# Hybrid attention and mLSTM encoder layer: ScalarE by hand in the attention stage, two normalizations shared by two engines, two mask additions moved

## The chip, the cores and the metric

The kernel runs on one core of one Trainium2 chip. The metric is the device time of one execution in microseconds (us), measured over several runs; lower is better.

## What is computed

One layer of an encoder on 2048 tokens of width 1024, in float32. The input is normalized, scaled and shifted by vectors made from a conditioning vector, and projected. The columns of the projection feed two groups of heads, whose outputs are normalized, concatenated, projected back, and followed by a SwiGLU feed-forward part. Cut to what matters here:

```python
hmix = rms_norm(x, g_norm1) * (1.0 + scale1) + shift1
q_a, k_a, v_a, q_m, k_m, v_m, o_m, gates = split(hmix @ w_in)
# 8 heads of 64 in two groups of 4; |t - s| <= 128, so a block of 128 queries sees up to 3 blocks of keys
logits = where(valid, scores - slopes * dist, -inf)
mx  = maximum(max(logits), sink)
p   = exp(logits - mx); den = sum(p) + exp(sink - mx)
att = rms_norm((p / den) @ v, g_attn_out)
# 4 heads of 128, chunks of 128, a forward and a backward scan, added
h_m = rms_norm(mlstm_forward + mlstm_backward, g_mlstm_out) * sigmoid(o_m)
x = x + gate1 * (concatenate([att, h_m]) @ w_out)
# then the feed-forward part and the last norm
```

## The kernel before

TensorE (PE) does all products; VectorE (DVE), ScalarE (ACT) and GpSimd (POOL) share the rest; loads and stores are issued by SyncE (SP). Products that need float32 accuracy are made of three: a factor is split into a half rounded to the format of the fast product (made by ACT) and the remainder (made by DVE or POOL). The stages follow one another: modulation and first norm with the natural projections, gates, mLSTM, attention, output projection, feed-forward part.

**What sets the order.** Each engine works through its own queue in order. The framework schedules: from the program it lets each engine take whatever its model of the time says is ready, the earlier emitted first, and so may move an instruction far ahead of where it was emitted. Inside `tc.manual_schedule(engines=...)` the engines named keep the order of emission. PE is under it everywhere; the gates and mLSTM stages, and the output projection, hold all engines under it; in the attention stage of the kernel before, ACT, DVE, POOL and SP are left to the scheduler.

**The filler.** Projection matmuls (`gps`, L498) are generators in a deque, `fill`; `pull(n)` emits `n` of them between the other matmuls. A tile of 128 columns by 512 tokens takes 24 matmuls, and when the generator is resumed after the 24th, it emits the eviction by ACT (`qhi` of `qk_att`, `oth` of `o_tiles`). `put_soon(k, ...)` emits an operation `k` pulls later. `cols_steps` makes the weights of such a tile: the load of `wraw` (L247; there is one such buffer), the rounded half `whi` by ACT (L251), and the remainder `wlo` in four parts by POOL (L254). `next_cols` spreads these steps over the pulls ahead of their use; `proj_cols` emits all of them at once. `o_tiles` calls `proj_cols` when its first tile begins:

```python
        if not ws_:
            ws_.extend(proj_cols(C_OM + h * P) for h in heads)
```

In the attention stage the filler is: the rest of the sigmoid gate's head 0 (`o_first`), one query tile column (`second`), head 1 (`o_tiles((1,), ...)`), and heads 2 and 3 together, in four blocks (`lasts`).

**Attention.** 32 units (one block of 128 queries, one group of four heads) pass through a loop over `s_` with three stages in flight: the newest unit's four scores with DVE's maximum (L786) and ACT's exponential (L788); the normalization (`normalize`: a small ACT exponential, L794, two small DVE operations, and four scalings by POOL, L798) and, for the unit before, PE transposes (L805) with their split into `apth` (ACT, L141) and `aptl` (DVE, L142); and for the unit before that the products with the values (L817, L818) and their eviction `at` (L821, L822). The loop also draws on `first_pair`, from `s_` = 21 on one step each time: it loads the first pair of row tiles for the output projection, squares them on ACT (L1139) with additions on POOL (L1141, L1143), starts the loads of the first two parts of the output weights `wo` as soon as the filler's first block of heads 2 and 3 is done, and gates. After the loop `finish_wo` emits the halves of these weights (ACT L1046, DVE L1047).

**mLSTM.** For each of four heads a backward pass over the chunks 15 to 1 builds the backward states (`k_chunk`, `kv_mm`), then a forward pass makes scores, states and products. `load_bc` loads the rows of a chunk (`bc`), `prep` adds the mask to them on POOL (L629), `decays` takes the exponential on ACT (L635), and `scores` uses that. `prep` of chunks 0 and 1 is emitted after the backward pass.

Of the kernel before, what the change touches and what calls it, by code (L numbers as in the profile page):

```python
# [11 lines left out]
F32 = mybir.dt.float32  # L12
# [3 lines left out]
AF = mybir.ActivationFunctionType  # L16
ALU = mybir.AluOpType
MUL, ADD, SUB, MAX, MIN = ALU.mult, ALU.add, ALU.subtract, ALU.max, ALU.min
# [18 lines left out]
def hybrid_layer_kernel(  # L37
# [5 lines left out]
    pe, dve, act, pool, sp = nc.tensor, nc.vector, nc.scalar, nc.gpsimd, nc.sync  # L43
# [72 lines left out]
    def beat(k=1):  # L116
        for e in soon:
            e[0] -= k
        due = [e for e in soon if e[0] <= 0]
        soon[:] = [e for e in soon if e[0] > 0]  # L120
        for _, f, args in sorted(due, key=lambda e: e[0]):
            f(*args)

    def pull(n=1):

        while n > 0:
            if not fill:
                n -= 1
                beat()
            elif next(fill[0], None) is None:  # L130
                fill.popleft()
            else:
                n -= 1
                beat()

    def finish_fill(g):
        while any(f is g for f in fill):
            pull()
# [436 lines left out]
    def tick():  # L575

        due = [f for k, f in later if k <= 0]
        later[:] = [[k - 1, f] for k, f in later if k > 0]
        for f in due:
            f()  # L580

    def load_v(h, n):
        va = s2.tile([P, 4, 129], F32, tag="mv", name="mv", bufs=2)
        sp.dma_start(va, vaug_d[n * 512:(n + 1) * 512, h, :].rearrange("(c p) d -> p c d", p=P))
        return va

    def load_qk(h, j, n):
        t = s2.tile([P, 512], F32, tag="mqk", name="mqk", bufs=4)
        sp.dma_start(t, qk_d[j, h, n])
        return t  # L590

    def load_last(h):
        return {NB - 1: (load_qk(h, 1, NB - 1), load_v(h, NB - 1))}

    def mlstm(h, nb, nf, last):
# [5 lines left out]
        def load_bc(cc):  # L601
            bc = s2.tile([P, 4, P], F32, tag="bc", name="bc", bufs=3)
            sp.dma_start(bc.rearrange("p j t -> p (j t)"), bc_d[h, cc].rearrange("j t -> (j t)").partition_broadcast(P))
            return bc
# [3 lines left out]
        def k_chunk(k_c, va_c, d, cc):  # L608
            kn = kns.get(cc)
            if kn is None:  # L610
                tp = bank("a", "ktp")
                pe.transpose(tp[:, :P], k_c, ident)
                kn = kns[cc] = s2.tile([P, P], F32, tag=f"kn{cc}", name="kn", bufs=1)
                act.activation(kn, tp[:, :P], AF.Copy)
            vw = s2.tile([P, 129], F32, tag="vw", name="vw", bufs=4)
            rr = row(d, cc)
            act.activation(vw, va_c, AF.Copy, scale=wT[:, rr:rr + 1])
            return kn, vw

        def kv_mm(kn, vw, tag="a"):  # L620
            kvp = bank(tag, "kvp")
            pe.matmul(kvp[:, :129], kn, vw, start=True, stop=True)  # L622
            return kvp
# [3 lines left out]
        def prep(cc):  # L627
            ng = ngs[cc] = s2.tile([P, 2, P], F32, tag="ng", name="ng", bufs=3)
            pool.tensor_tensor(ng, bcs[cc][:, 0:2, :], maskb, ADD)  # L629

        def decays(cc):

            for d in range(2):
                rr = row(d, cc)
                act.activation(ngs[cc][:, d, :], ngs[cc][:, d, :], AF.Exp, bias=rT[:, rr:rr + 1])  # L635
# [5 lines left out]
        for cc in list(range(NT - 1, 0, -1)) + [0, 0, 0]:  # L641
            tick()
            n, i = divmod(cc, 4)
            if i == 3 and n and n - 1 not in blk:
                blk[n - 1] = (load_qk(h, 1, n - 1), load_v(h, n - 1))
            if cc == 6:
                q_first = load_qk(h, 0, 0)
            if cc in (6, 4, 2):
                bcs[3 - cc // 2] = load_bc(3 - cc // 2)
            if cc:  # L650
                todo.append((cc, *k_chunk(blk[n][0][:, i * P:(i + 1) * P], blk[n][1][:, i, :], 1, cc)))
                pull(nb - nb // 2)
            if len(todo) > 2 or (todo and not cc):
                c_, kn, vw = todo.popleft()
                kvp = kv_mm(kn, vw, "bcdc"[c_ % len("bcdc")])
                if c_ == NT - 1:
                    dve.tensor_copy(cb[:, c_ - 1, :], kvp[:, :129])
                else:
                    rr = row(1, c_)
                    dve.scalar_tensor_tensor(cb[:, c_ - 1, :], cb[:, c_, :], dec[:, rr:rr + 1], kvp[:, :129], MUL, ADD)  # L660
                pull(nb // 2)
        prep(0)
        prep(1)
        decays(0)


# [74 lines left out]
        for cc in range(NT + 1):  # L741
            tick()
            if cc == NT - 3 and h + 1 < HM:
                last = load_last(h + 1)
# [24 lines left out]
    class Unit:  # L769
# [18 lines left out]
            act.activation(p[:, :NK], p[:, :NK], AF.Exp, bias=nm, scale=-1.0, accum_out=self.rs[:, g:g + 1])  # L788
            self.p.append(p)

        def normalize(self):
            dn = s3.tile([P, 4], F32, tag="adn", name="adn")
            dve.tensor_tensor(dn, self.nmx, skb[:, self.kv * 4:self.kv * 4 + 4], ADD)
            act.activation(dn, dn, AF.Exp)  # L794
            dve.tensor_tensor(dn, dn, self.rs, ADD)
            dve.reciprocal(dn, dn)
            for g in range(4):
                pool.tensor_scalar(self.p[g][:, :self.NK], self.p[g][:, :self.NK], dn[:, g:g + 1], 0.0, MUL, ADD)  # L798

        def transpose(self, i):  # L800
            if i >= self.nk:
# [177 lines left out]
    for i in range(2 * 96 + 60):  # L979
# [3 lines left out]
        if i == 150:  # L983
            t = s2.tile([P, 512], F32, tag="og", name="mqk", bufs=1)
            sp.dma_start(t, qk_d[1, 0, NB - 1])
            last = {NB - 1: (t, load_v(0, NB - 1))}
# [13 lines left out]
    for h in range(HM):  # L1000
        if h:
            for g in convs[h]:
                finish_fill(g)
        last = mlstm(h, 3, 11, last)
# [31 lines left out]
    wo = []  # L1036

    def start_wo(u):
        hl = [[big(4 * u + 2 * z + i, "wo") for i in range(2)] for z in range(2)]
        wo.append(hl)  # L1040
        for i in range(2):
            sp.dma_start(hl[1][i].bitcast(F32), wo_d[u, 2 * i:2 * i + 2].rearrange("k p t -> p k t"))

    def finish_wo(u):
        for hi, lo in zip(*wo[u]):
            act.activation(hi, lo.bitcast(F32), AF.Copy)  # L1046
            dve.tensor_tensor(lo, lo.bitcast(F32), hi.bitcast(F32), SUB)  # L1047

# [79 lines left out]
    def first_pair(cur):  # L1130

        cur.load_a()
        cur.load_m()
        cur.t = t = w0.tile([P, 4, P], F32, name="ms0")
        yield True
        for i in range(2):
            for k in (0, 2):
                yield True
                act.activation(t[:, 0:2], cur.a[:, i, k:k + 2], AF.Square)  # L1139
                f, g = (t[:, 0], t[:, 1]) if k == 0 else (t[:, 2 + i], t[:, 0])  # L1140
                pool.tensor_tensor(t[:, 2 + i], f, g, ADD)  # L1141
                if k:
                    pool.tensor_tensor(t[:, 2 + i], t[:, 2 + i], t[:, 1], ADD)  # L1143
        while lasts[0] in fill:
            yield True
        for u in range(2):
            start_wo(u)
        cur.load_gate()
        yield True
        yield True  # L1150
        cur.gate()

    nxt = Pair(0)
    chain0 = first_pair(nxt)
    order = [(bi, kv) for kv in range(KV) for bi in range(NT)]
    ahead = deque(att_loads(*o) for o in order[:2])
    pull(36)
    u1 = u2 = None
    for s_ in range(len(order) + 2):
        if s_ + 2 == NT:  # L1160
            for g in second:
                finish_fill(g)
            beat(1 << 20)
        u0 = None
        if s_ < len(order):
            u0 = Unit(*ahead.popleft())
        for g in range(4):
            if u0:
                u0.score(g)
            pull(1)  # L1170
            if u2 and g < 3:
                u2.values(g)
        if s_ + 2 < len(order):
            ahead.append(att_loads(*order[s_ + 2]))
        if u0:
            u0.normalize()
        pull(1)
        for i in range(3):
            if u1:
                u1.transpose(i)  # L1180
            pull(1 if i == 0 or i == 2 and s_ % 2 else 2)
        u2, u1 = u1, u0
        if s_ > 20:
            next(chain0, None)
    assert next(chain0, None) is None and len(wo) == 2
    finish_wo(0)
    finish_wo(1)
    s3s.close()


# [67 lines left out]
    for i in range(2):  # L1258
        columns(ps, i, sq[:, i])
    nx2.diagonal(rsqrt(mx, ps[:, :2], 2, 512, "ar"), diag())  # L1260
    finish_wo(2)
    finish_fill(lasts[2])
    for u in (4, 5):
# [217 lines left out]
    for p in range(NPR):  # L1481

        cur, nxt, nx2, xr0 = nxt, nx2, nx3, xr
# [480 lines left out]
```

## Time and profile before

| | |
|---|---|
| median of three runs | 2263.45 us (2263.4 to 2265.4) |
| profiled execution | 2268.64 us, of which the profile's span is 2266.8 |
| mean granted clock of TensorE in the profiled execution | 0.995 |
| busy: PE, DVE, ACT, POOL | 98%, 71%, 47%, 46% of the span |
| HBM | 269.95 MB read, 119.19 MB written |

In a timeline a row gives the start in us from the beginning of the span, the duration in us, the engine, the line of the kernel, the operation, the tiles written and read, the shape, how many such instructions the row joins, and in brackets how long the engine was idle before it and what ended that. PE's matmuls overlap, so that their starts tell more than their durations. In a table of windows, each engine has its busy time and count in the stretch; then come the granted clock of TensorE, the share of the DMA engines and GB/s.

### The profile page before, as it was taken

Reading aid. Unit: us, or ns where it says so; the run is one execution under the profiler, and the core shown is the slowest. Engines: PE = TensorE matmul, PEld = TensorE weight load, DVE = VectorE, ACT = ScalarE, POOL = GpSimd, SP = SyncE. Lnnn points to the kernel's source line nnn. Section 1 sums busy time; section 2 is a strip of 40 time slices with the busy share of each in tenths; the row PEclk is TensorE's granted clock in tenths of the full one; section 3 lists DMA queues with packets and bytes.
Section 4 is the critical chain, followed back from the end, with each engine's and each line's share of the span. In section 5 each row is a group of like instructions: output and inputs, shape, how many; then the busy total and the mean of one; then the engine's idle time right before and its main releaser. Section 6 shows DMA issues by size and latency. Waiting matters only on the chain.

```text
span 2266.8 us, 32424 instructions
## 1 busy us (share of the span) xinstructions
PE 2223.8 (98%) x10822; PEld 1858.7 (82%) x10822; DVE 1611.1 (71%) x2944; ACT 1060.3 (47%) x2206; POOL 1040.6 (46%) x914
## 2 busy tenths in 40 slices
PE   6999999999999999999999999999999999999998
PEld 4997888888888878888888888888888888878887
DVE  6787577656688877886767786766666665785694
ACT  5433565654677746354444444433333333233452
POOL 1006635334344333436666674457566654692020
PEclk9999999999999999999999999999999999999999
DMA  8476755586666576764343454433333374542462
GB/s 329 161 244 209 246 166 168 182 240 180 205 186 183 174 243 207 268 235 150 108 149 112 158 181 164 157 98 111 98 112 98 112 260 142 176 142 94 144 217 93
DMA packets 352811, 391.28 MB, mean 173 GB/s; under 512 B 21260, under 2 KB 251004, under 8 KB 352644
## 3 DMA queue, kind: packets, MB, share of 16 engines
q1 hardware_dynamic: 352420, 389.18, 52.6%
q8 instruction: 85, 1.39, 0.2%
q14 instruction: 82, 0.67, 0.1%
q10 hardware_dynamic: 224, 0.04, 0.0%
HBM read 269.95 MB, written 119.19 MB: 172 GB/s over the span
## 4 chain that ended last, share of the span: by engine, by line
PE 88%; DVE 4%; ACT 3%; DMA 2%; issue 1%; POOL 1%; SPq 0%; ACTq 0%; POOLq 0%; DVEq 0%
PE gps L498 14%; PE fp L56 12%; PE fp L57 12%; PE fp L58 12%; PE fo L56 6%; PE fo L58 6%; PE fo L57 6%; PE ops L56 2%; PE ops L58 2%; PE ops L57 2%; PE kvp L622 1%; PE num L709 1%; PE num L711 1%; PE atp L805 1%; ACT ap L788 1%
## 5 line engine op out<-in xcount | busy, mean ns | idle before, releaser
L498 PE MATMUL gps<-hT,whi 128*128 128x512 f32 x1088 | 396.5, 419 | 0.3 <-DVE cacc L513 0.3
L56 PE MATMUL fo<-w,ah 128*128 128x512 f32 x616 | 239.9, 389 | 1.0 <-DVE rb L1876 1.0
L58 PE MATMUL fo<-w,al 128*128 128x512 f32 x616 | 239.9, 389 | 0.1
L57 PE MATMUL fo<-w,ah 128*128 128x512 f32 x616 | 239.7, 389 | 0.0
L498 PE MATMUL gps<-hT,wlo 128*128 128x512 f32 x544 | 226.7, 417 | 0.0
L498 PEld LDWEIGHTS gps<-hT,whi 128*128 128x128 f32 x1088 | 200.2, 190 | 24.7 <-DVE cacc L513 0.7
L56 PE MATMUL fp<-T,S 128*128 128x512 f32 x528 | 206.7, 391 | 0.3 <-ACT s L1610 0.3
L57 PE MATMUL fp<-T,S 128*128 128x512 f32 x528 | 205.6, 389 | 0.0
L58 PE MATMUL fp<-T,S 128*128 128x512 f32 x528 | 205.4, 389 | 0.0
L1718 DVE TENSOR_TENSOR al<-al,ah 128x1024 fp32r<-128x1024 f32 x77 | 117.4, 1530 | 108.0 <-ACT ah L1717 108.0
L1717 ACT ACTIVATE ah<-al 128x1024 fp32r<-128x1024 f32 x77 | 81.6, 1060 | 182.8 <-DMA al<-a_d 180.3
L1453 DVE TENSOR_TENSOR S<-sf,S 128x512 fp32r<-128x512 f32 x86 | 129.8, 1547 | 34.4 <-ACT S L1452 34.2
L1453 DVE TENSOR_TENSOR A<-graw,A 128x512 fp32r<-128x512 f32 x86 | 130.8, 1541 | 13.2 <-ACT A L1452 12.8
L58 PE MATMUL fp<-B,A 128*128 128x512 f32 x352 | 136.9, 389 | 0.0
L56 PE MATMUL fp<-B,A 128*128 128x512 f32 x352 | 136.9, 389 | 0.0
L57 PE MATMUL fp<-B,A 128*128 128x512 f32 x352 | 136.9, 389 | 0.0
L56 PEld LDWEIGHTS fo<-w,ah 128*128 128x128 f32 x616 | 115.6, 188 | 25.4 <-DVE rb L1876 1.8
L58 PEld LDWEIGHTS fo<-w,al 128*128 128x128 f32 x616 | 115.6, 188 | 24.7 <-DVE al L1718 0.5
L57 PEld LDWEIGHTS fo<-w,ah 128*128 128x128 f32 x616 | 115.6, 188 | 24.2
L1620 DVE SCALAR_TENSOR_TENSOR g<-t,g 128x512 f32<-128x512 f32 x44 | 41.8, 950 | 131.3 <-ACT t L1619 131.3
L798 POOL TENSOR_SCALAR ap<-ap,adn 128x384 f32<-128x384 f32 (+1 forms) x128 | 73.5, 594 | 125.7 <-PE atp L805 58.6
L1457 POOL TENSOR_TENSOR sf<-A,A22r 128x512 f32<-128x512 f32 x42 | 58.1, 1383 | 145.5 <-DMA A22r<-in_w_ffn_in_dram 118.5
(427 smaller groups left out, 6142.2 us busy)
## 6 DMA issues: line engine op xcount, KB each, us to landing
al<-a_d SPq DMA_DIRECT2D x77, 512.0 KB, 3.8
wmod<-in_w_mod_dram SPq DMA_DIRECT2D x48, 512.0 KB, 7.6
graw<-in_w_ffn_in_dram SPq DMA_DIRECT2D x43, 512.0 KB, 3.9
a_d<-ka SPq DMA_DIRECT2D x66, 256.0 KB, 4.7
bc<-bc_d SPq DMA_DIRECT2D x64, 256.0 KB, 3.7
hop_d<-n SPq DMA_DIRECT2D x56, 256.0 KB, 4.0
a_d<-u SPq DMA_DIRECT2D x55, 256.0 KB, 4.6
mqk<-qk_d SPq DMA_DIRECT2D x44, 256.0 KB, 3.8
```

Source lines behind the costliest of these rows:

```text
L56: pe.matmul(o, lh, rh, start=first, stop=False, skip_group_check=skip)
L57: pe.matmul(o, lh, rl, start=False, stop=False, skip_group_check=skip)
L58: pe.matmul(o, ll, rh, start=False, stop=last, skip_group_check=skip)
L498: pe.matmul(ps, w[i == 2][:, k, :], hT[n](i == 1, k), start=(k == 0 and i == 0), stop=(k == KT - 1 and i == 2))
L622: pe.matmul(kvp[:, :129], kn, vw, start=True, stop=True)
L709: pe.matmul(num[:, d, :129], sc[:, d, :], va_c, start=True, stop=st is None)
L798: pool.tensor_scalar(self.p[g][:, :self.NK], self.p[g][:, :self.NK], dn[:, g:g + 1], 0.0, MUL, ADD)
L1453: dve.tensor_tensor(t[:, 1, :], f, t[:, 0, :].bitcast(F32), SUB)
L1457: add.tensor_tensor(f1, a21, a22, ADD)
L1620: dve.scalar_tensor_tensor(g0, t0, 1.0, g0, ADD, MUL)
L1717: act.activation(ah, al.bitcast(F32), AF.Copy)
L1718: dve.tensor_tensor(al, al.bitcast(F32), ah.bitcast(F32), SUB)
```

## The change

- Attention: the loop runs under `manual_schedule` for ACT, so ACT keeps the order of emission; DVE, POOL and SP stay with the scheduler.
- `first_pair` emits the halves of the first two parts of the output weights itself, one pair of tiles at a time, one step of the loop apart; `finish_wo(0)` and `finish_wo(1)` after the loop are gone.
- The first and the last unit's scalings are divided: heads 0 and 2 stay on POOL, heads 1 and 3 go to ACT.
- mLSTM: `prep` of chunks 0 and 1 is emitted in the backward pass, at chunks 3 and 1.

```diff
@@ mlstm
             if cc in (6, 4, 2):
                 bcs[3 - cc // 2] = load_bc(3 - cc // 2)
+            if cc in (3, 1):
+                prep(1 - cc // 2)
             if cc:
                 todo.append((cc, *k_chunk(blk[n][0][:, i * P:(i + 1) * P], blk[n][1][:, i, :], 1, cc)))
...
-        prep(0)
-        prep(1)
         decays(0)
@@ Unit
-        def normalize(self):
+        def normalize(self, last=False):
...
             for g in range(4):
-                pool.tensor_scalar(self.p[g][:, :self.NK], self.p[g][:, :self.NK], dn[:, g:g + 1], 0.0, MUL, ADD)
+                p = self.p[g][:, :self.NK]
+                if last and g % 2:
+                    act.activation(p, p, AF.Copy, scale=dn[:, g:g + 1])
+                else:
+                    pool.tensor_scalar(p, p, dn[:, g:g + 1], 0.0, MUL, ADD)
@@
+    def halves(hi, lo):
+        act.activation(hi, lo.bitcast(F32), AF.Copy)
+        dve.tensor_tensor(lo, lo.bitcast(F32), hi.bitcast(F32), SUB)
+
     def finish_wo(u):
         for hi, lo in zip(*wo[u]):
-            act.activation(hi, lo.bitcast(F32), AF.Copy)
-            dve.tensor_tensor(lo, lo.bitcast(F32), hi.bitcast(F32), SUB)
+            halves(hi, lo)
@@ first_pair
         for u in range(2):
             start_wo(u)
         cur.load_gate()
-        yield True
+        for u in range(2):
+            for hl in zip(*wo[u]):
+                yield True
+                halves(*hl)
         yield True
         cur.gate()
@@ the attention loop
     u1 = u2 = None
+    byhand = ExitStack()
+    byhand.enter_context(tc.manual_schedule(engines={mybir.EngineType.Activation}))
     for s_ in range(len(order) + 2):
...
         if u0:
-            u0.normalize()
+            u0.normalize(s_ in (0, len(order) - 1))
...
+    byhand.close()
     assert next(chain0, None) is None and len(wo) == 2
-    finish_wo(0)
-    finish_wo(1)
     s3s.close()
```

In `first_pair` the slot of the squares is also written with a variable `z`, which is 0: the same instructions.

More of the change, by code (lines that the diff above doesn't have):

```diff
@@ L1138, in first_pair @@
                 yield True
-                act.activation(t[:, 0:2], cur.a[:, i, k:k + 2], AF.Square)
-                f, g = (t[:, 0], t[:, 1]) if k == 0 else (t[:, 2 + i], t[:, 0])
+                z = 0
+                act.activation(t[:, z:z + 2], cur.a[:, i, k:k + 2], AF.Square)
+                f, g = (t[:, z], t[:, z + 1]) if k == 0 else (t[:, 2 + i], t[:, 0])
                 pool.tensor_tensor(t[:, 2 + i], f, g, ADD)
```

## The prediction

> **What bounds the kernel now.** I read the page first, then the windows of the two stages that the change touches, then the timelines of every engine there.
>
> ```profile
> span 2266.8 us, 32424 instructions
> PE 2223.8 (98%) x10822; PEld 1858.7 (82%) x10822; DVE 1611.1 (71%) x2944; ACT 1060.3 (47%) x2206; POOL 1040.6 (46%) x914
> PE 88%; DVE 4%; ACT 3%; DMA 2%; issue 1%; POOL 1%; SPq 0%; ACTq 0%; POOLq 0%; DVEq 0%
> ...
> 710.00:720.00 10.00, 9.00 (x51) 7.27 (x50) 6.39 (x19) 7.87 (x23) 4.16 (x9) 1.00 0.82 254
> ...
> 780.00:790.00 10.00, 8.85 (x48) 6.58 (x47) 7.39 (x18) 5.34 (x14) 5.27 (x7) 1.00 0.16 34
> ```
>
> TensorE (PE) is the bound: 98% busy, 88% of the chain. The change takes no matmul away, so it can only win waits of PE, or add some. In the windows the first pair is busy time and count of PE. Attention runs from about 584 to 793 us, and its two worst slices lose 1.00 and 1.15 us of 10. But a busy PE hides short waits, so I went to single instructions. Here is one attention unit, ScalarE (ACT) first, then PE:
>
> ```profile
> 652.66 0.62 ACT L788 ACTIVATE ap<-ap,nmx 128x384 f32<-128x384 f32 x1 [1.67 <-DVE nmx L786]
> 655.90 1.58 ACT L141 ACTIVATE apth<-atp 128x512 fp32r<-128x512 f32 x3
> 658.99 0.62 ACT L788 ACTIVATE ap<-ap,nmx 128x384 f32<-128x384 f32 x1 [1.51 <-DVE nmx L786]
> ...
> 656.93 0.39 PE L817 MATMUL ao<-apth,av 128*128 128x512 f32 x1
> 657.28 0.50 PE L818 MATMUL ao<-aptl,av 128*128 128x512 f32 x1
> ```
>
> The first exponential of a unit starts at 652.66, the first copy of transposed weights (apth) at 655.90, the next unit's first exponential at 658.99. So the loop exponentials, copies, VectorE's differences, VectorE's next maxima takes 6.33 us. PE's own work per unit is about as long: L818 starts 0.35 us after L817, where the same pair elsewhere (733.21 and 733.44, shown below) needs 0.23, so PE already waits a little for that loop. Hence the rule for the rest: what comes between exponentials and copies on ACT is soon paid by PE; what fits into ACT's 1.5 us of idleness ahead of a unit's first exponential is free.
>
> **Part 1: ScalarE in the order of emission.** For most ACT instructions the executed order of before already is the order of the loop: three exponentials, the output copy (L821), the fourth, the small one of the normalization, three copies; and counting PE's projection matmuls in 24s (its order is the program's) puts nearly all `oth` and `qhi` evictions where they are executed now. I take 0 for these. What is not at its place are the weight conversions `whi` (L251). `o_tiles` calls `proj_cols` at the moment its first tile begins: load, conversion on ACT, four subtractions on POOL, and the next matmul uses the result. In the kernel before, these run early, moved ahead by the scheduler. By hand they cannot. Head 1's tiles begin here:
>
> ```profile
> 662.43 0.70 PE L498 MATMUL gps<-hT,whi 128*128 128x512 f32 x2
> ...
> 664.16 1.09 ACT L251 ACTIVATE whi<-wraw 128x1024 fp32r<-128x1024 f32 x1
> 665.32 0.62 ACT L788 ACTIVATE ap<-ap,nmx 128x384 f32<-128x384 f32 x1
> ...
> 665.32 2.83 POOL L254 TENSOR_TENSOR wlo<-wraw,whi 128x256 fp32r<-128x256 f32 x4 [0.23 <-ACT whi L251]
> ...
> 668.18 0.38 SPq L247 DMA_DIRECT2D wraw<-in_w_in_dram  x1
> ```
>
> The matmul at 662.43 is the 1st of head 1's tiles (the 1345th of L498). The `whi` at 664.16 is head 2's, done a whole head early; its subtractions end at 668.15 and free the only `wraw` buffer, and at 668.18 head 3's load goes out. After the change head 1's conversion stands at just this place, behind the last `qhi`, and PE waits for it: from 662.43 to 665.25, 2.8 us. Behind PE stand the next unit's scores. They come 2.8 us later, at 665.8, their maximum takes 0.6, so the exponential of 665.32 moves to about 666.9, by 1.5 us only; the loop regains 1.3 us on PE, which spares PE later waits like that at 657.28. Price: 1.5 to 2.8, I take **1.8**.
>
> Heads 2 and 3 begin together, 96 matmuls later, with both conversions emitted one behind the other:
>
> ```profile
> 726.23 0.39 PE L498 MATMUL gps<-hT,whi 128*128 128x512 f32 x1
> 733.21 0.39 PE L817 MATMUL ao<-apth,av 128*128 128x512 f32 x1
> 733.44 0.46 PE L818 MATMUL ao<-aptl,av 128*128 128x512 f32 x1
> ...
> 727.61 1.08 ACT L251 ACTIVATE whi<-wraw 128x1024 fp32r<-128x1024 f32 x1
> 728.76 0.62 ACT L788 ACTIVATE ap<-ap,nmx 128x384 f32<-128x384 f32 x1
> ...
> 728.77 2.83 POOL L254 TENSOR_TENSOR wlo<-wraw,whi 128x256 fp32r<-128x256 f32 x4 [0.22 <-ACT whi L251]
> ...
> DMA to landing us min/median/max: 4.2/5.6/6.1
> ```
>
> As it was, the `whi` at 727.61 is head 3's. After, head 2's takes that place and ends at 728.7. Head 3's follows at once on ACT, but its load needs `wraw`, which POOL's subtractions for head 2 hold until 728.77 + 2.83 = 731.6. The load lands 4.2 to 5.6 us later (last row, all 17 `wraw` loads), at 735.8 to 737.2; with 1.05 us of conversion ACT is free at 736.9 to 738.3. All that time ACT stands still, with a unit's four exponentials, its output copy, the normalization's exponential and three copies queued behind it. PE first waits 2.4 us for head 2's conversion (726.23 to 728.7), works through one unit, for which everything is there, and then stands at the product of 733.21. That needs the copy behind four exponentials: 655.90 − 652.66 = 3.24 us after ACT goes on, and 0.6 long, so 740.7 to 742.1. PE comes 7.5 to 8.9 us later than 733.21, with up to 0.4 for the second difference. I take **8.3**, the 2.4 included.
>
> To the good stands one place, the squares for the output's norm (L1139):
>
> ```profile
> 712.88 0.44 ACT L1139 ACTIVATE ms<-ma 128x256 f32<-128x256 f32 x1
> ...
> 716.13 0.60 ACT L788 ACTIVATE ap<-ap,nmx 128x384 f32<-128x384 f32 x1
> ...
> 720.00 0.50 PE L817 MATMUL ao<-apth,av 128*128 128x512 f32 x1 [0.95 <-ACT apth L141]
> 720.73 0.50 PE L818 MATMUL ao<-aptl,av 128*128 128x512 f32 x1 [0.23 <-DVE aptl L142]
> ```
>
> Three of them ran in a row from 712.88, each behind POOL's additions for the one before, ahead of the exponential of 716.13. PE paid with 0.95 us of idleness ahead of 720.00, and 0.73 from there to 720.73 where 0.23 would do: 1.5 us. By hand one square goes to the end of each of four units, into ACT's idle 1.5 us: **−1.5**, at worst 0 (the loop then stays near its edge). The four `halves` of 1.05 us, one at the end of each of units 29 to 32, go into the same idleness, at nothing; without it each would cost its 1.05.
>
> **Part 2: normalization on two engines, first and last unit.**
>
> ```profile
> 589.57 0.62 ACT L788 ACTIVATE ap<-ap,nmx 128x384 f32<-128x384 f32 x1 [0.77 <-DVE nmx L786]
> 590.52 1.52 PE L805 MATMUL atp<-ident,ap 128*128 128x128 f32 x4
> ...
> 784.10 0.50 ACT L788 ACTIVATE ap<-ap,nmx 128x256 f32<-128x256 f32 x1
> 785.86 2.81 POOL L798 TENSOR_SCALAR ap<-ap,adn 128x256 f32<-128x256 f32 x4 [3.40 <-DVE adn L796]
> 787.81 1.24 PE L805 MATMUL atp<-ident,ap 128*128 128x128 f32 x3 [0.41 <-POOL ap L798]
> ```
>
> First unit: four transposes take 1.52 us, for they follow POOL's four scalings one by one; with half of these on ACT a little over half of it goes, some 0.9. But ACT's two (some 0.5 each, by the exponential of 784.10, which has that shape) stand ahead of the exponential of 589.57 and push the second unit's copies back by about 1.0. I take 0, between −0.9 and +0.5. Last unit: ACT's fourth exponential came late (784.10, behind copies), so POOL's 2.81 us end at 788.67, with PE waiting at 787.81. By hand that exponential isn't behind copies and the scaling is shared: up to all of the 1.15 us that PE loses in the slice of 780 to 790 goes. Against it, two scalings of 0.5 stand on ACT ahead of the previous unit's copies. **−0.5**, from −1.2 to +1.
>
> **Part 3: mLSTM, the additions of the mask (`prep`, L629) earlier.**
>
> ```profile
> 340.47 0.73 POOL L254 TENSOR_TENSOR wlo<-wraw,whi 128x256 fp32r<-128x256 f32 x1 [9.71 <-PE kvp L622]
> 341.16 1.42 POOL L629 TENSOR_TENSOR ng<-bc,maskb 128x256 f32<-128x256 f32 x2
> 341.94 0.69 ACT L635 ACTIVATE ng<-ng,rT 128x128 f32<-128x128 f32 x2 [1.54 <-POOL ng L629]
> 343.14 0.49 PE L622 MATMUL kvp<-vw,kn 128*128 128x129 f32 x2 [1.22 <-ACT vw L617]
> 334.73 0.42 SPq L603 DMA_DIRECT2D bc<-bc_d  x1
> bc<-bc_d SPq DMA_DIRECT2D x64, 256.0 KB, 3.7
> ```
>
> In head 1 the two additions stand on POOL behind a subtraction that waits for a conversion; ACT waits 1.54 for them, PE 1.22 for ACT. Emitted at the third and the last step of the backward pass, they go ahead of it: the first bias row lands at 334.73 + 3.7 = 338.4, and POOL is idle then. In the three other heads PE shows no wait of this kind. **−1.2**, from −1.4 to 0.
>
> **Sum.** 1.8 + 8.3 − 1.5 − 0.5 − 1.2 = +6.9 us. The profiled execution took 2268.6 (span 2266.8, 1.8 around it), so 2275.5; the median of the three runs, 2263.45, lies 5.2 lower: **2270 us**.
>
> **The rivals.**
>
> (a) The conversions don't stop ACT, because they still run early or the slack behind them is larger than I read. For it: I read the order from the code and from counted matmuls, not from a run. Then the gains stand alone: −3.2, and with the loop relieved, small waits like that at 657.28 (0.12 us; over 32 units some 3.8) may go: 2257 to 2260, so 2258. It decides if PE's 1st matmul of head 1 doesn't wait. Chance 0.17.
>
> (b) The halt is there but half of it is regained: a load at 4.2 us or less, all gains at their best. +2, so 2265. Chance 0.10.
>
> (c) PE's clock falls in the halt.
>
> ```profile
> 836.00:837.00 1.00, 1.00 (x4) 0.90 (x5) 0.00 (x0) 0.00 (x0) 1.00 (x2) 0.50 0.00 0
> 836.85 0.63 PE L57 MATMUL ops<-wo,mS 128*128 128x512 f32 x1
> 837.27 0.63 PE L58 MATMUL ops<-wo,mS 128*128 128x512 f32 x1
> ```
>
> After pauses from 829 to 836 the granted clock (the third number from the end) is 0.50 here, and matmuls start 0.42 us apart in place of 0.23, for ten of them: 2 us. My halt at 733.21 holds PE still for 5 to 6 us without a break; +2.0 makes 2272. Against it: ACT and VectorE, the loop that PE then runs against, aren't slowed, so a part is hidden. Chance 0.13. [...]
>
> (d) As forecast: 0.60, in its own range 2266 to 2275.
>
> **How the numbers follow.** A measurement of this kernel can tell about 0.2%, 4.5 us, from no change: 2258.9 to 2268.0. Of (a) most lies below, so faster 0.12; the rest of it, (b) and the forecast's lower edge make same 0.18; the forecast and (c) make slower 0.70. The range 2259 to 2276 leaves out the most of (a) and the far end of (c).
>
> **What would show it.** Right: `whi` at the start of heads 1 and 2, and one ACT wait for the `wraw` load of 7 to 9 us, with PE idle 5 us behind it; no three squares in a row; no POOL wait of L635 in head 1. Wrong: `whi` executed a head early as now, or PE's 1st matmul of head 1 in step with the transposes before it.

## The result and the profile after

Six runs each: before 2264.94 us median (2263.40 to 2267.22), after 2278.92 (2275.77 to 2284.39). The ratio is 1.0062, 95% interval 1.0052 to 1.0072: slower by 14.0 us. The forecast was 2270.0 in a range of 2259 to 2276. The direction was right, the forecast was about half of the measured size, and the range was missed.

The first lines of the page of after, and its costliest group:

```profile
span 2274.8 us, 32425 instructions
PE 2225.4 (98%) x10822; PEld 1860.8 (82%) x10822; DVE 1602.2 (70%) x2944; ACT 1062.5 (47%) x2210; POOL 1037.1 (46%) x910
...
PE 89%; DVE 4%; ACT 3%; DMA 2%; issue 1%; POOL 0%; SPq 0%; ACTq 0%; DVEq 0%; POOLq 0%
...
L498 PE MATMUL gps<-hT,whi 128*128 128x512 f32 x1088 | 396.5, 419 | 5.2 <-ACT whi L251 5.0
```

The shares look as before. What is new stands in the last line: 5.0 us in which PE waited for a weight conversion by ACT. Two windows of after, the same as shown of before:

```profile
710.00:720.00 10.00, 9.96 (x57) 8.34 (x56) 7.76 (x25) 8.32 (x24) 2.27 (x4) 1.00 0.69 203
780.00:790.00 10.00, 8.82 (x47) 6.74 (x46) 9.34 (x23) 7.70 (x18) 2.96 (x6) 1.00 0.32 81
```

The slice with the three squares (710 to 720) has lost its idleness: PE is busy for 9.96 of 10 where it was 9.00. The other one still loses 1.18.

Windows don't add up to a difference of two kernels, but matmuls do: PE executes the same 10822 in the same order in both, so the start of the n-th in one trace can be taken from the start of the n-th in the other. This lag (after minus before) says where time was lost. At before's times it reads:

| before, us | lag, us | what lies between | step |
|---|---|---|---|
| 330 | −2.7 | (ahead of the change: chance of the two executions; in the traces of the other versions this lag lies between −2.9 and +3.5) | |
| 345 | −3.4 | mask additions of head 1 | −0.8 |
| 661 | −1.9 | first unit and the loop behind it | +1.5 |
| 700 | +2.4 | head 1's conversion | +4.3 |
| 722 | +0.8 | squares | −1.6 |
| 745 | +8.0 | heads 2 and 3: both conversions | +7.2 |
| 780 | +9.8 | units 29 to 32, with conversions of output weights | +1.8 |
| 830 | +10.3 | the rest of these, last unit | +0.4 |
| 845 | +11.0 | start of the output projection | +0.7 |

The steps from 330 to 845 make +13.7, close to the measured +14.0. The spans differ by less, 8.0, because the profiled execution of before had lost 2.7 us by chance ahead of the change, and after's made up 3.0 behind 860, where both kernels are the same. Both profiled executions lie off their medians accordingly: before's 2268.64 is 3.7 above, after's 2276.64 is 2.3 below.

The two halts in after's timeline (PE, ACT, POOL and SP rows; columns as before):

```profile
662.25 1.08 ACT L251 ACTIVATE whi<-wraw 128x1024 fp32r<-128x1024 f32 x1
663.39 0.72 PE L498 MATMUL gps<-hT,whi 128*128 128x512 f32 x2 [2.61 <-ACT whi L251]
...
728.41 1.08 ACT L251 ACTIVATE whi<-wraw 128x1024 fp32r<-128x1024 f32 x1
729.55 0.69 PE L498 MATMUL gps<-hT,whi 128*128 128x512 f32 x1 [2.36 <-ACT whi L251]
729.58 2.79 POOL L254 TENSOR_TENSOR wlo<-wraw,whi 128x256 fp32r<-128x256 f32 x4 [0.24 <-ACT whi L251]
...
732.39 0.37 SPq L247 DMA_DIRECT2D wraw<-in_w_in_dram  x1
735.78 1.06 ACT L251 ACTIVATE whi<-wraw 128x1024 fp32r<-128x1024 f32 x1 [6.29 <-DMA wraw<-in_w_in_dram]
...
740.62 0.50 PE L821 MATMUL ao<-apth,av 128*128 128x512 f32 x1 [2.25 <-ACT apth L141]
```

This is the mechanism of the forecast: head 1's conversion waits at its first tile with PE behind it (2.61); then head 2's (2.36), POOL's subtractions hold the only `wraw`, head 3's load goes out when they end (732.39), ACT stands for 6.29 us in front of it with a unit's exponentials and copies behind, and PE arrives at the product at 740.62. Before, that product stood at 733.21. One thing is not in the forecast. The windows of after behind the first of these waits:

```profile
664.00:665.00 1.00, 1.00 (x6) 0.85 (x5) 0.39 (x1) 0.00 (x0) 1.00 (x3) 0.92 0.92 203
665.00:666.00 1.00, 1.00 (x4) 0.91 (x4) 0.24 (x2) 0.71 (x2) 1.00 (x2) 0.50 1.01 213
666.00:667.00 1.00, 1.00 (x3) 0.77 (x3) 0.63 (x2) 0.21 (x1) 0.22 (x1) 0.50 0.06 14
667.00:668.00 1.00, 1.00 (x4) 0.94 (x3) 0.00 (x0) 0.50 (x2) 0.00 (x0) 0.50 0.50 131
668.00:669.00 1.00, 1.00 (x6) 0.81 (x5) 0.63 (x2) 0.29 (x1) 0.00 (x0) 0.87 1.13 340
```

The granted clock (third number from the end) is halved from 664.8 to 668.3. PE is busy, but with 3 or 4 matmuls per microsecond in place of 6. Of head 1's +4.3, 1.4 came here; the same after 729.55 (window 731 to 732: 0.50) gave 1.4. After the wait of 2.25 at 740.62 the clock stayed full.

The first unit, in PE's rows, before's and then after's:

```profile
593.82 0.40 PE L817 MATMUL ao<-apth,av 128*128 128x512 f32 x1
594.06 0.40 PE L818 MATMUL ao<-aptl,av 128*128 128x512 f32 x1
```

```profile
590.15 0.50 PE L821 MATMUL ao<-apth,av 128*128 128x512 f32 x1 [0.47 <-ACT apth L141]
591.25 0.50 PE L822 MATMUL ao<-aptl,av 128*128 128x512 f32 x1 [0.60 <-DVE aptl L142]
```

The shared scalings gain 0.9 us on the transposes, but ACT's two stand ahead of the next exponential, so that copies and differences are late: 0.24 between the two products became 1.10, with 0.47 of waiting in front. Of the +1.5 in the table, 0.7 are there by 600; the other 0.8 come in the loop behind it. The last unit in after:

```profile
781.38 1.36 DVE L1050 TENSOR_TENSOR wo<-wo 128x1024 fp32r<-128x1024 f32 x1
790.17 1.32 DVE L1050 TENSOR_TENSOR wo<-wo 128x1024 fp32r<-128x1024 f32 x1
794.24 0.91 ACT L800 ACTIVATE ap<-ap,adn 128x256 f32<-128x256 f32 x2 [0.51 <-DVE adn L796]
795.82 0.50 PE L821 MATMUL ao<-apth,av 128*128 128x512 f32 x1 [1.45 <-ACT apth L141]
```

ACT's two scalings (0.91) stand ahead of the copy for which PE then waits 1.45. And the differences of the output weights (L1050, 1.3 us each) stand on VectorE between maxima and differences of the units.

Mask additions of head 1 in after:

```profile
337.73 0.74 POOL L629 TENSOR_TENSOR ng<-bc,maskb 128x256 f32<-128x256 f32 x1 [9.64 <-DMA bc<-bc_d]
338.51 0.69 ACT L635 ACTIVATE ng<-ng,rT 128x128 f32<-128x128 f32 x2 [0.78 <-POOL ng L629]
339.71 0.49 PE L622 MATMUL kvp<-vw,kn 128*128 128x129 f32 x2 [0.43 <-ACT vw L617]
```

POOL had been idle for 9.64 us until the rows landed, and no subtraction stands in front any more. ACT's wait shrank from 1.54 to 0.78, PE's from 1.22 to 0.43.

### The profile page after: what moved, and what is told of

Its sections match the earlier page's. It is cut to its first block, busy times and chain, and to the rows that moved or that the text cites. A ratio compares the mean times of both kernels' runs of the same rounds, so it can differ in the third digit from the quotient of the medians.

```text
span 2274.8 us, 32425 instructions
## 1 busy us (share of the span) xinstructions
PE 2225.4 (98%) x10822; PEld 1860.8 (82%) x10822; DVE 1602.2 (70%) x2944; ACT 1062.5 (47%) x2210; POOL 1037.1 (46%) x910
## 4 chain that ended last, share of the span: by engine, by line
PE 89%; DVE 4%; ACT 3%; DMA 2%; issue 1%; POOL 0%; SPq 0%; ACTq 0%; DVEq 0%; POOLq 0%
PE gps L498 14%; PE fp L56 12%; PE fp L57 12%; PE fp L58 12%; PE fo L56 6%; PE fo L57 6%; PE fo L58 6%; PE ops L56 2%; PE ops L58 2%; PE ops L57 2%; PE num L709 1%; PE kvp L622 1%; PE atp L809 1%; PE num L711 1%; PE ao L822 1%
```

## The experiments

All comparisons are with the kernel before on the same chip. Experiments that ran on different chips are compared with each other only through it. A ratio of 0.001 is 2.3 us. Most intervals are 0.001 wide to each side, so two versions that differ by under about 0.0014 are not told apart by their times alone; there the traces carry the argument, and one trace is one execution.

**1. Is it ScalarE's order?** `sched_act` takes the order back to the scheduler:

```diff
-    byhand.enter_context(tc.manual_schedule(engines={mybir.EngineType.Activation}))
```

> The changed kernel with one thing undone: ScalarE is left to the scheduler again in the attention loop; the shared normalizations, the weights' halves in the loop and the mask additions stay. Theory O (order): by hand, the weight conversions of heads 1 to 3 come at their use and halt PE twice, 4.3 and 7.1 us by the two traces laid beside each other; with the scheduler they run early again, so most of the 14 us comes back: 2263 to 2268, no PE wait for whi. Theory N (normalization and halves): the shared scalings and the halves at the stage's end cost most; those stay here, so 2272 or more.

Measured 0.9993 [0.9984, 1.0002]. The whole loss goes with this line; what is left of the change gains at most a little.

**2. Do the halts carry it?** `early_weights` keeps the order by hand, but emits the weights of heads 1, 2 and 3 long before their use:

```diff
-    wo23 = []
+    wo1, wo23 = [], []
...
-    fill.extend([o_tiles((1,), range(NB), [])] + lasts)
+    fill.extend([o_tiles((1,), range(NB), wo1)] + lasts)
...
+        if s_ in (2, 12, 22):
+            (wo1 if s_ == 2 else wo23).append(proj_cols(C_OM + (s_ // 10 + 1) * P))
```

> The changed kernel, ScalarE still by hand, with the weights of heads 1, 2 and 3 emitted at the ends of units 2, 12 and 22, the places where the kernel before executed them. Theory O: both halts and the halved clock behind them go, 11.4 us: 2266 to 2269; no PE wait for whi, and no ScalarE wait for wraw in attention. Theory N: ScalarE by hand is not the cost, and this gives back 3 us at most: 2275 to 2279.

Measured 1.0030 [1.0018, 1.0042]. No PE wait for `whi` is left, yet only about 7 of the 14 us are back, which lies between the two theories. The timeline of early_weights has a new wait:

```profile
771.07 1.23 DVE L1102 SCALAR_TENSOR_TENSOR mm<-og,mm 128x1024 f32<-128x1024 f32 x1 [1.85 <-DMA og<-og_d]
...
772.96 0.50 PE L822 MATMUL ao<-aptl,av 128*128 128x512 f32 x1 [2.65 <-DVE aptl L142]
```

VectorE, whose order nobody touched, now has the output gate (L1102) ahead of a unit's differences, and waits 1.85 for the load of `og`; PE pays 2.65. The scheduler orders VectorE by its model of the time, and with the weights elsewhere it came out otherwise.

**3. Two loads or two conversions?** `third_apart` emits head 3's weights only when head 3's own first tile begins, so that ACT doesn't stand in front of a load:

```diff
-        if not ws_:
-            ws_.extend(proj_cols(C_OM + h * P) for h in heads)
         for n in blocks:
-            for h, w in zip(heads, ws_):
+            for z, h in enumerate(heads):
+                if z == len(ws_):
+                    ws_.append(proj_cols(C_OM + h * P))
+                w = ws_[z]
```

> The changed kernel, but head 3's weights are emitted when its own first tile begins, 24 projection matmuls after head 2's, and not directly behind head 2's. Theory O (a conversion at its use halts PE, whether its load is there or not): ScalarE's wait of 6.3 us for the load goes, but a third short halt of 2.5 to 4 us comes at head 3's first tile, so little changes: 2275 to 2279. Theory L (only the wait for the load costs; a conversion whose load is there is nearly free): 7 us come back: 2271 to 2273.

Measured 1.0068 [1.0055, 1.0080], about 1 us above the range of theory O. PE's waits in third_apart:

```profile
PE gps L498 <- ACT whi L251: 8.2, 3, 3.2
```

Three waits in place of two. It is no better than after: what costs is the conversion at the time of use, with or without the long wait for its load.

**4. The clock behind the short pauses.** `busy_pause` puts eight dummy matmuls, whose result is overwritten, ahead of head 1's first tile and of heads 2 and 3's:

```diff
+            idle = 8
+        else:
+            idle = 0
...
+                for _ in range(idle):
+                    pe.matmul(ps, hT[n](0, 0, slice(0, P)), hT[n](0, 0), start=True, stop=True)
+                idle = 0
```

> The changed kernel with eight matmuls more (their result is overwritten) ahead of the first tile of head 1 and again of heads 2 and 3, where PE would stand for 2.4 to 2.6 us; they need nothing that is waited for, and take 8 x 0.23 = 1.85 us out of the pause. Theory C (PE's clock): the granted clock stays at 1.00 behind both pauses, and the slower matmuls there (1.3 and 1.4 us) are gained: 2275 to 2277.5. Theory H (hidden): PE runs against the loop of ScalarE and VectorE behind the pauses anyway, so a full clock changes nothing: 2278 to 2280.

Measured 1.0074 [1.0061, 1.0087], above both expectations at its median. Windows of busy_pause:

```profile
746.00:747.00 1.00, 1.00 (x4) 0.90 (x4) 0.74 (x2) 0.70 (x3) 1.00 (x2) 0.50 0.25 45
666.00:667.00 1.00, 1.00 (x6) 0.78 (x6) 1.00 (x2) 1.00 (x3) 1.00 (x3) 1.00 0.91 307
731.00:732.00 1.00, 1.00 (x6) 0.83 (x5) 1.00 (x3) 1.00 (x4) 1.00 (x3) 1.00 0.93 306
```

The clock stays full at 666 and 731, but PE comes earlier to the product that waits for ACT, stands there, and then the clock is halved (746). The product in its timeline (L827 in this kernel):

```profile
744.88 0.50 PE L827 MATMUL ao<-apth,av 128*128 128x512 f32 x1 [4.54 <-ACT apth L141]
```

Keeping PE busy in the short pauses only moved the price to the long one here.

**5. The mask additions alone.** `mask_alone` is the kernel before with that one edit:

```diff
+            if cc in (3, 1):
+                prep(1 - cc // 2)
...
-        prep(0)
-        prep(1)
```

> The kernel before with the mask additions of the change and nothing else. Prediction: PE's wait of 1.2 us in head 1 goes, nothing else moves: 1.2 us less (the steps at this place in the traces so far are 0.5 to 1.35), ratio 0.9994 to 0.9998. Rival: the time saved is lost again where the heads' next waits are (POOL or the loads of bc): ratio 1.0000.

Measured 0.9997 [0.9988, 1.0006]: −0.9 us at its median. It fits −1.2 and can't be told from nothing by the times. In its trace the step at that place is −1.2.

**6. The gate's place.** `early_gate` is early_weights with the output gate emitted behind the loop:

```diff
-        yield True
-        cur.gate()
...
+    nxt.gate()
     nx2, nx3 = Pair(1), Pair(2)
```

> early_weights with the gate of the first pair (VectorE, 1.2 us) emitted behind the attention stage. Theory G: in early_weights the scheduler put that gate on VectorE's queue ahead of the differences of unit 29, where it waited 1.85 us for its load, and PE paid 2.7 us; that goes here: 2.5 us under early_weights, ratio to before about 1.0019. Rival: another operation waits there for the same DMA traffic, and the time stays: 1.0030.

Measured 1.0030 [1.0020, 1.0040], but this tells nothing about the gate: VectorE isn't under the order by hand, and the scheduler put the gate back where it was. The edit did not do what it says.

**7. First and last unit.** On the base of early_gate, `early_all` gives the first unit's scaling back to POOL alone, `gate_pool` the last unit's too:

```diff
-            u0.normalize(s_ in (0, len(order) - 1))
+            u0.normalize(s_ in (len(order) - 1,))   # early_all; gate_pool: s_ in ()
```

> early_gate with the first unit's scalings all on POOL again (the last unit's stay shared). Theory F: ScalarE's two scalings of the first unit push the second unit's exponentials and copies back, and cost 1.2 to 1.5 us net; ratio to before 1.0013 or less, 0.0006 under early_gate. Rival: PE waits for POOL's scalings as before and nothing is gained: equal to early_gate.

> early_gate with the first and the last unit's scalings all on POOL. Theory F with a last unit that pays as I predicted (0.5 us gained by sharing): 0.5 us over early_all. Rival: sharing the last unit costs, since the two scalings stand on ScalarE ahead of unit 30's copies (PE waits 1.45 us there in the changed kernel): 0.5 to 1.5 us under early_all.

Measured 1.0016 [1.0007, 1.0025] and 1.0013 [1.0004, 1.0022], with early_gate's 1.0030 on the same chip. By the times, the first unit's sharing costs 0.0014 (3.2 us) without the halts, and the last unit's neither gains nor costs. The traces say otherwise. At the first unit PE gains 0.7 us in early_all; another 1.6 come later, between 791.0 and 794.4, and what brings them was not shown. At the last unit, PE's wait for the copy shrinks from 1.61 in early_all to 0.20 in gate_pool, and PE is 1.4 us earlier there: by hand, sharing the last unit costs 1.4. The times hide it, because in gate_pool the wait of experiment 2 is 1.0 longer:

```profile
772.49 1.23 DVE L1102 SCALAR_TENSOR_TENSOR mm<-og,mm 128x1024 f32<-128x1024 f32 x1 [2.89 <-DMA og<-og_d]
...
774.37 0.50 PE L822 MATMUL ao<-aptl,av 128*128 128x512 f32 x1 [3.63 <-DVE aptl L142]
```

**8. That wait taken away at its cause.** `og_first` is gate_pool with the load of `og` ahead of the four weight loads; `early_og` does the same to early_weights, with nothing else undone:

```diff
+        cur.load_gate()
         for u in range(2):
             start_wo(u)
-        cur.load_gate()
```

> The version with early weights and both normalizations on POOL (ratio 1.0013), with the load of the output gate (og) issued ahead of the four weight loads in place of behind them. In that version's trace the gate on VectorE waits 2.89 us for og, with the differences of a unit queued behind it, and PE comes 3.70 us later there. Theory G (that wait on VectorE is the price): og is there in time, the step of 3.70 at that place goes, ratio 0.9995 to 1.0003. Rival S (VectorE is merely late there, and the gate's place does not matter): 1.0010 to 1.0016. If the weight loads come later by the reordering and the halves wait, 1.002 or more.

> The changed kernel with two edits: the weights of heads 1, 2 and 3 emitted at the ends of units 2, 12 and 22, and the load of the output gate ahead of the four weight loads, so that VectorE does not wait for it. Both halts are gone without the gate's wait in their place. If the halts cost the 11.4 us that the two traces show at their places: 1.0010 to 1.0014. If a part is given back later without them (about 9 us, by the sum of the runs so far): 1.0018 to 1.0023.

og_first: 1.0004 [0.9996, 1.0013], against gate_pool's 1.0013: just above the range of theory G, and not told apart by the times. The gate still waits 1.43 us for `og`, at 769.04, but that comes earlier, and in the trace the step at the product is gone: its lag against gate_pool falls by 3.4 us there, of which 1.2 had been lost just ahead. early_og: 1.0015 [1.0006, 1.0024]. That leaves 0.0047 of 0.0062 to the halts, 10.6 us, close to the 4.3 + 7.2 = 11.5 of the table. In the traces early_og gains 11.3 us on after at these two places, and gives some 3 back at units 29 to 32. In early_og's timeline the gate waits at 768.86, a little earlier, and what is left of it falls on a copy:

```profile
768.86 1.23 DVE L1102 SCALAR_TENSOR_TENSOR mm<-og,mm 128x1024 f32<-128x1024 f32 x1 [1.54 <-DMA og<-og_d]
...
770.77 0.47 PE L821 MATMUL ao<-apth,av 128*128 128x512 f32 x1 [1.14 <-ACT apth L141]
```

**9. The conversions of the output weights.** `halves_end` is gate_pool with the four conversions emitted behind the loop, where ACT is the scheduler's again; `after_halves` does it in the changed kernel; `og_halves` is og_first with it:

```diff
-        for u in range(2):
-            for hl in zip(*wo[u]):
-                yield True
-                halves(*hl)
...
     byhand.close()
+    finish_wo(0)
+    finish_wo(1)
```

> The same version, with the four conversions of the output weights and their differences emitted behind the loop in place of one at the end of each of units 29 to 32. Theory H (they are not hidden: in the changed kernel's trace PE falls back by 0.35, 0.62, 0.52 and 0.65 us beside them, on ACT and on VectorE): 2.1 us less, ratio 1.0000 to 1.0007, unless the last ones then come late for the first output product. Rival F (they lie in idleness and cost nothing, as the prediction had it): 1.0011 to 1.0016.

> The changed kernel with one edit: the four conversions of the output weights emitted behind the loop, where ScalarE's order is the scheduler's again. The prediction had the four at the ends of units 29 to 32 at nothing: by it 1.0060 to 1.0064. Theory H (PE falls back by 0.35, 0.62, 0.52 and 0.65 us beside them): 1.0050 to 1.0056.

> ScalarE by hand, with early weights, og's load ahead of the weight loads, both normalizations on POOL alone, and the output weights' conversions behind the loop: the four places found so far are undone together. If ScalarE's order by hand costs nothing else: as with the scheduler's order, 0.9988 to 0.9998. If some 2 us of it lie elsewhere in the loop: 1.0000 to 1.0006.

halves_end: 1.0001 [0.9993, 1.0010], 0.0012 better than gate_pool, as theory H said; but its trace gives another reason. The scheduler moved the conversions up into the loop (757.7 to 769.5) and the gate behind them (777.48, no wait): the 3.3 us gained are those of the gate's wait. after_halves: 1.0075 [1.0061, 1.0088], above after by as much as the times can just tell, against both expectations. Its timeline:

```profile
784.84 1.06 ACT L1049 ACTIVATE wo<-wo 128x1024 fp32r<-128x1024 f32 x1 [0.85 <-DMA wo<-wo_d]
...
786.36 1.23 DVE L1102 SCALAR_TENSOR_TENSOR mm<-og,mm 128x1024 f32<-128x1024 f32 x1 [1.74 <-DMA og<-og_d]
...
788.31 0.74 PE L822 MATMUL ao<-aptl,av 128*128 128x512 f32 x1 [1.15 <-DVE aptl L142]
```

Here the scheduler put the conversion and the gate where their loads weren't there yet. og_halves: 1.0001 [0.9993, 1.0010], no better than halves_end, since the weights, now loaded behind `og`, are late for ACT:

```profile
771.25 1.06 ACT L1049 ACTIVATE wo<-wo 128x1024 fp32r<-128x1024 f32 x1 [1.57 <-DMA wo<-wo_d]
...
773.07 0.50 PE L821 MATMUL ao<-apth,av 128*128 128x512 f32 x1 [2.26 <-ACT apth L141]
```

So theory H, a price of 2.1 us for the emission at these places, isn't shown: PE falls back by 1.8 us at these units, but both ways of moving the conversions have a price too.

**10. The first unit in the changed kernel itself.** `after_first` takes back only its sharing:

```diff
-            u0.normalize(s_ in (0, len(order) - 1))
+            u0.normalize(s_ in (len(order) - 1,))
```

> The changed kernel with one edit: the first unit's scaling on POOL alone again (the last unit's stays on both engines). The prediction's step put the first unit's sharing at 0, between -0.9 and +0.5 us: by it the ratio stays within 1.0060 to 1.0064. Theory F (it costs 1.4 us of trace at its place, and 0.0014 by the runs with early weights): 1.0046 to 1.0056. If the halts ahead take the loss up, 1.0062.

Measured 1.0060 [1.0048, 1.0073], against 1.0062: nothing, and not the 0.0014 of experiment 7 (the intervals would still allow it). The trace of after_first shows why the gain doesn't stay. Against after, PE loses the 0.9 us at the transposes and gains 1.6 at the products behind them, 0.7 net; it gains another 1.6 and 1.5 us behind the short pauses at 664 and 730, where the clock now stays full. Then it stands longer at the product, and the clock falls there. The product in the timeline, and then windows of after_first:

```profile
739.64 0.49 PE L821 MATMUL ao<-apth,av 128*128 128x512 f32 x1 [4.14 <-ACT apth L141]
```

```profile
666.00:667.00 1.00, 1.00 (x7) 0.87 (x6) 0.59 (x3) 0.65 (x3) 0.35 (x1) 1.00 0.18 39
731.00:732.00 1.00, 1.00 (x6) 0.88 (x6) 0.63 (x2) 0.00 (x0) 0.10 (x1) 1.00 0.00 0
742.00:743.00 1.00, 1.00 (x4) 0.81 (x3) 0.44 (x2) 0.52 (x1) 0.24 (x1) 0.50 0.00 0
```

As in busy_pause, what is gained ahead of the long halt is lost in it.

**11. The scheduler's order with less sharing.** `sched_last` is sched_act with the first unit on POOL alone, `sched_pool` with both units on POOL alone:

```diff
-    byhand.enter_context(tc.manual_schedule(engines={mybir.EngineType.Activation}))
...
-            u0.normalize(s_ in (0, len(order) - 1))
+            u0.normalize(s_ in (len(order) - 1,))   # sched_last; sched_pool: s_ in ()
```

> The changed kernel with ScalarE's order left to the scheduler (ratio 0.9993) and the first unit's scaling on POOL alone; the last unit's stays on both engines. If the first unit's sharing costs under the scheduler what it cost by hand (0.0014): 0.9979 to 0.9985. If the scheduler places ACT's two scalings so that they cost nothing: 0.9990 to 0.9995.

> The changed kernel with ScalarE's order left to the scheduler and both units' scaling on POOL alone: only the move of the mask's additions and the new places of emission of the halves are left of the change. Prediction's step for the last unit (sharing gains 0.5, at most 1.2): 0.0002 to 0.0005 above the version that shares the last unit alone. Rival (sharing the last unit gains nothing, as by hand): equal to it, within 0.0003.

sched_last: 0.9986 [0.9977, 0.9995], the one version here whose interval lies below 1, by 3.2 us at its median; it is the best of sixteen, and the interval clears 1 by little. sched_pool: 0.9993 [0.9984, 1.0002]. The difference between the two has the sign of the prediction's step for the last unit, and is within the intervals. In sched_last the order is the scheduler's; its lag against before falls by 1.2 us at the mask and by 1.5 from 780 to 790, at the last unit. sched_pool falls there by 0.7: under the scheduler's order, sharing the last unit gains 0.8 in the traces, where by hand it cost 1.4.

## Why the prediction was right in direction and half in size

**Right.** ScalarE's order by hand is the cause, and mostly through the conversions at the time of use: experiments 1, 2, 3 and early_og. Rival (a), no halt, is out: PE's first matmul of head 1 waits 2.61. So is (b), half of the halt regained. The chain of heads 2 and 3 came as worked out, load after POOL's subtractions, ACT's wait, copy at the end: forecast +8.3, trace +7.2. ACT's wait was 6.29, where 7 to 9 were foreseen, because this load landed 3.4 us after its issue and not 4.2 to 5.6. Squares: −1.5, trace −1.6. Mask: −1.2, trace −0.8 here, and −1.0 to −1.5 at the same place in the traces of the other versions; ACT's wait for POOL is halved, not gone, since the rows land late.

**The step that failed first: head 1.** Forecast +1.8, trace +4.3. The wait was sized well (2.8 against 2.6), but "the loop regains 1.3 us on PE" did not happen: in after_first, where the clock stays full at this place, the step is +2.9, and nothing of it comes back up to 700. In after another 1.4 us came on top, because the clock was halved behind the wait. The prediction had looked for the clock only at the long halt, rival (c), and there on top of 5 to 6 us of standing. In fact PE stood there for 2.25: a part of the halt had been used up at half speed before. The trace of before had a hint: the clock was halved there from 834.0 on, and none of PE's pauses between 829 and 836 is longer than 2.09 us, so the clock had fallen there with short pauses alone ahead of it. busy_pause and after_first show that these belong together: with a full clock before it, PE stands 4.1 to 4.5 us at the product and the clock falls afterwards.

**The terms set at nothing.** The first unit came out at +0.7 in the trace, where the range was −0.9 to +0.5. ACT's two scalings delayed the next unit's exponentials and with them copies and differences: PE gained 0.9 at the transposes and fell back by 0.6 and 0.9 us at the two products shown. In the changed kernel, taking it back gained nothing measurable (after_first), so that this term and the halts do not simply add.

The loop behind the first unit lost 0.8 between 600 and 661, and after_first, which doesn't share the first unit, lost the same 0.8 there. The prediction had put ACT's evictions "nearly all" at their old places and taken 0 for them. But by hand one `qhi` eviction stands at 613.21, between three exponentials and the output copy, where before had it at 613.68, ahead of the unit's first exponential: by the prediction's own rule PE pays for that soon, and 0.4 of the 0.8 come at the next products. The other 0.4, in small steps up to 651, were not traced to an instruction.

Units 29 to 32, with the four conversions "into the same idleness, at nothing", lost 1.8 us. Of these, 0.4 come ahead of the first conversion (780.27), behind an `oth` eviction that now stands at 769.39 among the exponentials; 1.4 are left for the conversions. The price named without cover was 1.05 for each, 4.2 in all; a third of it came. The cover was counted on ACT alone: VectorE's differences of 1.3 us that go with each conversion had no such idleness. That these 1.4 us could be had back by another place of emission was not shown (experiment 9).

The last unit came out at +0.4 in place of −0.5. The forecast had taken order and sharing as gains together, against two scalings ahead of copies. In gate_pool, with the order by hand and no sharing, PE gains 0.9 on before at this place; the sharing takes 1.4 back (experiment 7).

**The range.** Its upper end, 2276, took rival (c) and the upper bounds of the halt, but not the ends of several small terms together: +2.5 (head 1), +0.7 and +0.8 (first unit and loop), +1.8 (units 29 to 32), +0.9 (last unit) and +0.4 (mask), less 1.1 on the halt of heads 2 and 3, are 6.0 of the 6.8 between forecast and table. Another 0.7 fell at the start of the output projection, which the forecast had no term for, and I take that for chance: the clock is halved there in both kernels, from 833.98 to 840.81 in before and from 845.75 to 852.58 in after, which, less the lag of 10.25 at this point, is 1.5 us later in PE's work. The matmuls that start 0.23 us apart behind 841 in before therefore start 0.42 apart in after. In the other versions' traces this step lies between −0.6 and +0.7.

**Open.** With all four places undone (og_halves, 1.0001) the order by hand is 0.0008 above sched_pool. The intervals don't separate them, and the one wait of 2.26 in og_halves' trace would be enough for it.

## What to carry to other kernels

Before an engine's queue is put in the order of emission, list the operations that its scheduler had moved far ahead of their place, above all those that need a load or feed another engine's next step; each can become a halt unless its emission is moved too. A queue by hand can also change the order of the queues that stay with the scheduler, and an edit there may do nothing or open a new wait, so look up the place of the moved instruction in the trace before reading the time. When a term is covered by one engine's idleness, ask the same of every engine that the operation brings with it.

## What had not been expected of the hardware

Behind pauses of PE of 2.25 to 2.65 us the clock was halved in some places and full in others. It was halved after waits of 2.61 and 2.36 us in after, 2.60 in third_apart and 2.26 in og_halves; it stayed full after 2.65 in early_weights, 2.39 in third_apart and 2.25 in after. Behind four longer waits, 3.21 in third_apart, 3.63 in gate_pool, 4.14 in after_first and 4.54 in busy_pause, it was halved. In after, gate_pool, after_first and busy_pause it was down for 3.4 us each time, behind the 3.21 in third_apart for at least 5.3 (0.50 in each window from 756 to 761, 0.83 in the next): in the five windows of after shown, the shortfalls 0.08 + 0.50 + 0.50 + 0.50 + 0.13 make 1.71 us, which at half speed is 3.42 us.

So the length of the pause alone does not tell these places apart: after 2.65 us the clock was full, after 2.26 it was not. What else decides was not shown. In after the halved clock added 1.4 us to each of the waits of 2.61 and 2.36, and nothing to the 2.25.
